# The opening's loads in one queue: weights in order of use on SyncE, a later pair on ScalarE

## Chip, cores, metric

The kernel runs on one core of one Trainium2 chip. The metric is the device time of one execution in microseconds (us); the median of three runs before the change is 1103.35 us (1103.25 to 1103.62). One more execution was profiled; times inside the kernel, counted from the start of its span, are from that one.

## The reference

One layer over x (256 tokens x 2048 features, float32): a norm, a combined projection, two kinds of attention with 8 heads each, a projection back, and a feed-forward block with a short convolution.

```python
h = rms_norm(x, attn_norm)
proj = h @ w_in                                    # 2048 x 6152
out_a = forgetting_attention(...)                  # 8 heads of 128
out_b = stick_breaking_attention(...)              # 8 heads of 128
x = x + concat(rms_norm(out_a), rms_norm(out_b)) @ w_out
u = conv3(rms_norm(x) @ w_up)
x = x + (silu(gate(u)) * val(u)) @ w_down
```

## The kernel before

Every float32 product is made of three products of a two-part split: a matrix is rounded to a high part on ScalarE or VectorE, VectorE subtracts it from the original for the low part, and TensorE adds up high by high, low by high and high by low.

The change lies in `opening()`, which computes the first 512 columns of `h @ w_in` for all 256 tokens. The weights of this product are 16 row tiles of 128 x 512 float32 (256 KB each), here called W0 to W15; x comes in column pieces of 128 features for both halves of the tokens, x0 to x15 (256 KB for two of them). The product runs in eight steps, c = 0 to 7; step c uses the weight tiles 2c and 2c+1 and the x pieces of the same numbers.

`load_x(k, n)` (L90) issues one DMA for the pieces k to k+n-1, always on SyncE's (SP's) queue. `load_w(c, which, queue)` (L391) issues one DMA for the pair c, or for one tile of it where `which` is given, on SP's queue or the queue named. Three buffers `w_raw` hold two pairs each: W0 to W3, W4 to W7, W8 to W11, then the first again.

`keep_busy(n)` (L379) issues n matmuls of zeros into a bank that nothing reads. `columns` (L126) turns the norm's weights, 16 x 128 in `prow`, into one value for each partition (`ga`): a transpose on TensorE and a copy on VectorE. `transposed_split` (L133) transposes x pieces on TensorE; ScalarE scales them by `ga` into the high part of `hT` (L143) and VectorE makes the low part (L146). `split_w(c)` (L402) makes `w_hi` and `w_lo` of pair c. In step 0 each tile is taken by itself: W0's cast is VectorE's (L409), W1's is ScalarE's (L418). In step 1 VectorE casts both tiles (L415); from step 2 on ScalarE casts the pair at once (L418). All `w_lo` are VectorE's (L419). `multiply(c, i, n, high)` (L423) issues the matmuls (L428): eight with the high weights for a pair, then four with the low ones.

The order of TensorE, VectorE, ScalarE and SP in the opening is that of the code (`manual_schedule`, L476): on each engine, instructions stand as the program issues them, and each engine runs its own in order. A DMA issue is an instruction of the queue's engine, so one on ScalarE stands between its casts. A DMA signals its end on one of eight semaphores, which are given out in turn; when all eight have been used, the next issue also waits until the earlier transfer with its semaphore has landed.

After the opening come the other projection columns by `token_major` (L237), whose weights go through the same three buffers on SP's queue (L200), attention, and the feed-forward block.

Of the kernel before, what the change touches and what calls it, by code (L numbers as in the profile page):

```python
# [18 lines left out]
KT = D // P  # L19
# [26 lines left out]
def hybrid_layer(  # L46
# [19 lines left out]
    nc = tc.nc  # L66
# [11 lines left out]
    def f32(t):  # L78
        return t.bitcast(F32)
# [4 lines left out]
    prow = const.tile([50, P], F32, name="prow")  # L84
# [5 lines left out]
    def load_x(k, n):  # L90
        nc.sync.dma_start(x2[:, :, k * P : (k + n) * P], xp[:, :, k * P : (k + n) * P])
# [29 lines left out]
    ga = const.tile([P, KT], F32, name="ga")  # L121
# [4 lines left out]
    def columns(dst, rows, n):  # L126
        pp = psb.tile([P, 512], F32, name="pp", tag="t")
        nc.tensor.transpose(pp[:, :n], rows, ident[:n, :n])
        dve.tensor_copy(dst, pp[:, :n])
# [3 lines left out]
    def transposed_split(k, g, n=2):  # L133

        ps = psb.tile([P, 2, S], F32, name="ps_x", tag="t")
        for j in range(n):
            for t in range(NT):
                nc.tensor.transpose(  # L138
                    ps[:, j, t * P : (t + 1) * P], xt[t][:, (k + j) * P : (k + j + 1) * P], ident
                )  # L140
        for j in range(n):
            i = k + j
            act.activation(hT[:, i, 0, :], ps[:, j, :], AF.Identity, scale=g[:, i : i + 1])  # L143
        for j in range(n):
            i = k + j
            dve.scalar_tensor_tensor(  # L146
                hT[:, i, 1, :], ps[:, j, :], g[:, i : i + 1], f32(hT[:, i, 0, :]),
                op0=ALU.mult, op1=ALU.subtract,
            )

    def sums_of_squares(ss, c, tiles=range(NT)):

        for t in tiles:
            junk = late.tile([P, 512], F32, name="junk", tag="raw", bufs=4)
            act.activation(junk, xt[t][:, c * 512 : (c + 1) * 512], AF.Square, accum_out=ss[:, t, c : c + 1])
# [62 lines left out]
    def rows_of(w, k0, n, c0, cols):  # L218
        return w[k0 * P : (k0 + n) * P, c0 : c0 + cols].rearrange("(k p) c -> p k c", p=P)
# [14 lines left out]
    def of_half(h, part, t):  # L234
        return h[:, part, t * P : (t + 1) * P]
# [51 lines left out]
    with ExitStack() as actx:  # L287
# [91 lines left out]
        def keep_busy(n):  # L379
            for _ in range(n):  # L380
                nc.tensor.matmul(idle, zeros[:, :P], zeros, start=True, stop=True)
# [3 lines left out]
        def opening():  # L385

            acc = psa.tile([P, NT, 512], F32, name="acc", tag="acc")
            pairs = [[(0, 1), (1, 1)]] + [[(0, 2)]] * 7
            raws, parts = [], []

            def load_w(c, which=None, queue=nc.sync):  # L391

                if c == len(raws):
                    raw = wraw.tile([P, 2048], F32, name="w_raw", tag="w_raw")
                    raws.extend([raw[:, :1024], raw[:, 1024:]])
                for i, n in [(which, 1)] if which is not None else [(0, 2)]:
                    queue.dma_start(
                        raws[c][:, i * 512 : (i + n) * 512].rearrange("p (a b) -> p a b", a=n),
                        rows_of(wi, 2 * c + i, n, 0, 512),
                    )  # L400

            def split_w(c):  # L402
                hi = whi.tile([P, 2048], F32R, name="w_hi", tag="w_hi")
                lo = wlo.tile([P, 2048], F32R, name="w_lo", tag="w_lo")
                parts.append([t[:, :1024].rearrange("p (a b) -> p a b", a=2) for t in (hi, lo)])
                for i, n in pairs[c]:
                    cols = slice(i * 512, (i + n) * 512)
                    if c == i == 0:
                        dve.tensor_copy(hi[:, cols], raws[c][:, cols])  # L409
                        for k in range(2):  # L410
                            transposed_split(k, ga, 1)
                    elif c == 1:
                        for j in range(2):
                            half = slice(512 * j, 512 * (j + 1))
                            dve.tensor_copy(hi[:, half], raws[c][:, half])  # L415
                        transposed_split(2, ga)
                    else:
                        act.copy(hi[:, cols], raws[c][:, cols])  # L418
                    dve.tensor_tensor(  # L419
                        lo[:, cols], raws[c][:, cols], f32(hi[:, cols]), op=ALU.subtract  # L420
                    )

            def multiply(c, i, n, high):  # L423
                hi, lo = (p[:, i : i + n] for p in parts[c])
                order = [(j, l, hi) for j in range(n) for l in range(2)] if high else [(j, 0, lo) for j in range(n)]
                for m, (j, l, r) in enumerate(order):
                    for t in range(NT):
                        nc.tensor.matmul(  # L428
                            acc[:, t, :], of_half(hT[:, 2 * c + i + j], l, t), r[:, j, :],
                            start=high and c == i == m == 0, stop=not high and c == 7 and m == n - 1,  # L430
                        )

            load_x(0, 2)
            nc.scalar.dma_start(prow[:KT, :], attn_norm[0].rearrange("(n p) -> n p", p=P))
            act.preload_act_table_set("natural_log_exp_and_others")
            load_w(0, 0)
            load_w(0, 1, nc.scalar)
            load_x(2, 2)
            load_w(1, 0, nc.scalar)
            load_w(1, 1)  # L440
            load_x(4, 2)
            load_w(2)
            load_x(6, 2)
            load_w(3)
            load_x(8, 4)
            load_w(4)
            load_x(12, 4)
            load_w(5)
            keep_busy(14)
            columns(ga, prow[:KT, :], KT)  # L450
            split_w(0)
            keep_busy(4)

            def behind(c):
                if c:
                    transposed_split(2 * c + 2, ga)
                split_w(c + 1)

            multiply(0, 0, 1, True)
            multiply(0, 1, 1, True)  # L460
            behind(0)
            sums_of_squares(ss1, 0, [0])
            multiply(0, 0, 1, False)
            multiply(0, 1, 1, False)
            for c in range(1, 8):
                if c < 7:
                    behind(c)
                sums_of_squares(ss1, c // 2, [c % 2])
                if c == 2:
                    load_w(6)  # L470
                    load_w(7)
                multiply(c, 0, 2, True)
                multiply(c, 0, 2, False)
            return acc

        with tc.high_priority(offset=AHEAD), tc.manual_schedule(  # L476
            engines={mybir.EngineType.PE, mybir.EngineType.DVE, mybir.EngineType.Activation, mybir.EngineType.SP}
        ):
            acc_q0 = opening()
# [695 lines left out]
```

## Time and profile before

| | |
|---|---|
| median of three runs | 1103.35 us |
| the profiled execution | 1103.81 us |
| its span | 1102.0 us |
| TensorE matmul busy | 1096.5 us (99%) |
| VectorE / ScalarE / GpSimd busy | 877.7 / 701.9 / 44.4 us |
| chain that ended last | PE 99% |
| data moved | 245.89 MB, 223 GB/s over the span |

The rows name an engine (PE is TensorE, PEld its weight loads, DVE VectorE, ACT ScalarE, POOL GpSimd, SP SyncE; SPq and ACTq are DMA issues), a line of the kernel, the operation and its operands, written tile first. An idle time in brackets lies just ahead of a row's first instruction, with what ended it. Numbers ahead of an engine are its start and its length in us. Rows of stretches give, for each engine, the busy time and the number of instructions, then the granted TensorE clock (1.00 is full), the DMA engines' mean busy share and the GB/s that they moved.

### The profile page before, as it was taken

How to read it: one execution, taken by the hardware profiler on the slowest of the kernel's cores; microseconds unless marked ns; L12 is line 12 of the kernel's file. 1: busy time of each engine (PE TensorE's matmuls, PEld its weight loads, DVE VectorE, ACT ScalarE, POOL GpSimd, SP SyncE). 2: the span in 40 equal slices, each digit the busy share in tenths (PEclk: the TensorE clock that was granted, in tenths of full speed). 3: DMA queues.
4: the chain of work that ended last, by engine and by line, in shares of the span. 5: the costliest groups of instructions: out<-in, count | busy, mean ns of one | idle time of the engine just before them, and what ended most of it. 6: DMA issues, size and time to landing. Idle time of an engine off the chain costs nothing.

```text
span 1102.0 us, 14826 instructions
## 1 busy us (share of the span) xinstructions
PE 1096.5 (99%) x5868; PEld 951.2 (86%) x5868; DVE 877.7 (80%) x941; ACT 701.9 (64%) x879; POOL 44.4 (4%) x46
## 2 busy tenths in 40 slices
PE   9999999999999999999999999999999999999998
PEld 7998888888888888888888888888888888888887
DVE  5655777975775677689889988889798889889896
ACT  6544556664653566677767776767676777677753
POOL 0000000000000000000000010100000010100010
PEclk9999999999999999999999999999999999999999
DMA  8776654576545396558989597986979689997985
GB/s 288 171 244 230 188 156 153 153 231 197 184 161 186 112 317 196 181 191 209 288 223 312 191 234 264 261 269 177 315 209 303 217 218 282 241 266 198 322 208 177
DMA packets 179407, 245.89 MB, mean 223 GB/s; under 512 B 4432, under 2 KB 119018, under 8 KB 179082
## 3 DMA queue, kind: packets, MB, share of 16 engines
q1 hardware_dynamic: 162458, 209.67, 58.6%
q0 software_dynamic: 16560, 34.75, 16.8%
q8 instruction: 46, 0.75, 0.3%
q10 hardware_dynamic: 320, 0.53, 0.1%
q14 instruction: 23, 0.19, 0.0%
HBM read 242.82 MB, written 2.11 MB: 222 GB/s over the span
## 4 chain that ended last, share of the span: by engine, by line
PE 99%; DMA 0%; DVE 0%; SPq 0%; issue 0%
PE pu L254 34%; PE acc L229 22%; PE pu L260 18%; PE bank_a L229 10%; PE bank_b L229 5%; PE bank_c L229 2%; PE acc L428 2%; PE acc L1053 1%; PE ps_x L138 1%; PE ps_o L593 1%; PE bank_a L1053 1%; PE ps_p L607 0%; DMA w_raw<-in_w_in_dram 0%; PE ps_o L594 0%; PE ps_h L307 0%; PE ps_s L522 0%
## 5 line engine op out<-in xcount | busy, mean ns | idle before, releaser
L208 DVE TENSOR_TENSOR w_lo<-w_raw,w_hi 128x2048 fp32r<-128x2048 f32 (+1 forms) x196 | 439.6, 2246 | 129.5 <-ACT w_hi L207 128.6
L207 ACT CAST w_hi<-w_raw 128x2048 fp32r<-128x2048 f32 (+1 forms) x196 | 367.3, 1877 | 235.9 <-PE acc L229 66.6
L254 PE MATMUL pu<-hT,w_hi 128*128 128x512 f32 x1664 | 394.0, 390 | 0.0
L254 PEld LDWEIGHTS pu<-hT,w_hi 128*128 128x128 f32 x1664 | 310.3, 188 | 63.2
L260 PEld LDWEIGHTS pu<-hT,w_lo 128*128 128x128 f32 x1664 | 211.9, 191 | 7.0
L260 PE MATMUL pu<-hT,w_lo 128*128 128x256 f32 x1664 | 215.1, 283 | 0.0
L229 PE MATMUL acc<-w_hi,hT 128*128 128x512 f32 (+1 forms) x576 | 124.5, 368 | 0.0
L229 PEld LDWEIGHTS acc<-w_hi,hT 128*128 128x128 f32 x576 | 101.5, 188 | 14.3
L207 ACT CAST w_hi<-w_sum 128x2048 fp32r<-128x2048 f32 x30 | 57.3, 1909 | 44.2 <-PE pu L254 36.6
L208 DVE TENSOR_TENSOR w_lo<-w_sum,w_hi 128x2048 fp32r<-128x2048 f32 x30 | 68.7, 2290 | 20.8 <-ACT w_hi L207 20.7
L870 ACT ACTIVATE tap<-up,ccol 128x256 f32<-128x256 f32 x176 | 74.6, 495 | 0.0
L229 PE MATMUL acc<-w_lo,hT 128*128 128x512 f32 (+1 forms) x288 | 64.6, 366 | 0.0
L229 PEld LDWEIGHTS acc<-w_lo,hT 128*128 128x128 f32 x288 | 51.6, 188 | 7.5
L975 POOL DMA_DIRECT2D w_sum<-in_w_down_dram x20 | 25.7, 1284 | 797.7 <-DVE w_lo L208 786.1
L229 PE MATMUL acc<-w_hi,oT 128*128 128x512 f32 x192 | 46.0, 392 | 0.0
L229 PEld LDWEIGHTS acc<-w_hi,oT 128*128 128x128 f32 x192 | 35.7, 188 | 7.3
L229 PE MATMUL bank_a<-w_hi,g 128*128 128x512 f32 x160 | 40.0, 392 | 0.0
L229 PE MATMUL bank_b<-w_hi,s 128*128 128x512 f32 x160 | 40.0, 392 | 0.0
L229 PE MATMUL bank_a<-w_hi,s 128*128 128x512 f32 x160 | 40.0, 392 | 0.0
L229 PEld LDWEIGHTS bank_b<-w_hi,s 128*128 128x128 f32 x160 | 28.9, 189 | 5.2
L229 PEld LDWEIGHTS bank_a<-w_hi,g 128*128 128x128 f32 x160 | 28.8, 189 | 5.3
L229 PEld LDWEIGHTS bank_a<-w_hi,s 128*128 128x128 f32 x160 | 28.9, 189 | 5.2
(211 smaller groups left out, 1068.7 us busy)
## 6 DMA issues: line engine op xcount, KB each, us to landing
w_raw<-in_w_up_dram SPq DMA_DIRECT2D x88, 1024.0 KB, 7.5
w_raw<-in_w_down_dram SPq DMA_DIRECT2D x44, 1024.0 KB, 6.4
w_raw<-in_w_in_dram SPq DMA_DIRECT2D x36, 1024.0 KB, 5.4
w_sum<-in_w_down_dram POOLq DMA_DIRECT2D x20, 1024.0 KB, 9.9
w_raw<-in_w_out_dram SPq DMA_DIRECT2D x16, 1024.0 KB, 5.1
w_raw<-in_w_down_dram POOLq DMA_DIRECT2D x10, 1024.0 KB, 14.9
w_raw<-in_w_in_dram SPq DMA_DIRECT2D x12, 688.0 KB, 4.2
w_raw<-in_w_in_dram SPq DMA_DIRECT2D x6, 512.0 KB, 6.8
```

The source lines that it names most:

```text
L138: nc.tensor.transpose(ps[:, j, t * P : (t + 1) * P], xt[t][:, (k + j) * P : (k + j + 1) * P], ident)
L207: act.copy(hi[:, :n], raw[:, :n])
L208: dve.tensor_tensor(lo[:, :n], raw[:, :n], f32(hi[:, :n]), op=ALU.subtract)
L229: nc.tensor.matmul(o, lhs(i, l, t), r[:, i, :], start=starts and j == 0, stop=stops and j == 3 * n - 1, skip_group_check=more,)
L254: nc.tensor.matmul(acc[:, j, :], hi[:, i, j * P : (j + 1) * P], hT[:, k].rearrange("p a b -> p (a b)"), start=k == 0, stop=low_first and k ...
L260: nc.tensor.matmul(acc[:, j, S:], lo[:, i, j * P : (j + 1) * P], hT[:, k, 0, :], start=False, stop=not low_first and k == KT - 1,)
L428: nc.tensor.matmul(acc[:, t, :], of_half(hT[:, 2 * c + i + j], l, t), r[:, j, :], start=high and c == i == m == 0, stop=not high and c == ...
L593: nc.tensor.matmul(po, v[j][:, hs], wp[:, k], start=i == 0, stop=False)
L870: act.activation(taps[w][:, j, :], u[:, j, w : w + S], AF.Copy, scale=ccol[:, w, f : f + 1])
L975: nc.gpsimd.dma_start(mem[into][:, : nk * 512].rearrange("p (a b) -> p a b", a=nk), src, accum_op=ALU.add)
L1053: nc.tensor.matmul(o, of_half(g, l, t), r[:, i, c0 : c0 + cols], start=kh == 0 and j == 0, stop=kh == n - 1 and j == 11,)
```

## The change

Only the order of the opening's loads, their queues and one idle matmul are changed. W1 and W2 go from ScalarE's queue to SP's, in the order in which they are used. The pair W4, W5 goes from SP's queue to ScalarE's, and its issue is moved behind ScalarE's part of step 0. The norm's weights stay the first issue of ScalarE's queue. `keep_busy(4)` ahead of the first product becomes `keep_busy(3)`.

```diff
-            load_x(0, 2)
             nc.scalar.dma_start(prow[:KT, :], attn_norm[0].rearrange("(n p) -> n p", p=P))
             act.preload_act_table_set("natural_log_exp_and_others")
+            load_x(0, 2)
             load_w(0, 0)
-            load_w(0, 1, nc.scalar)
+            load_w(0, 1)
             load_x(2, 2)
-            load_w(1, 0, nc.scalar)
+            load_w(1, 0)
+            load_x(4, 2)
             load_w(1, 1)
-            load_x(4, 2)
-            load_w(2)
             load_x(6, 2)
+            keep_busy(14)
+            columns(ga, prow[:KT, :], KT)
+            split_w(0)
+            keep_busy(3)
+            load_w(2, queue=nc.scalar)
             load_w(3)
             load_x(8, 4)
             load_w(4)
             load_x(12, 4)
             load_w(5)
-            keep_busy(14)
-            columns(ga, prow[:KT, :], KT)
-            split_w(0)
-            keep_busy(4)
```

SP's instructions before, from the first load on. The 128x2x256 rows are x0-1, x2-3, x4-5 and x6-7; the 128x512 rows W0 and W3; then come W4-5, x6-7, W6-7, x8-11, W8-9, x12-15 and W10-11. DMAHW0 to 7 are the eight semaphores (the ending is the same in every row):

```order
L91 DMA x_73<-in_x_dram 128x2x256
L397 DMA w_raw<-in_w_in_dram 128x512
L91 DMA x_73<-in_x_dram 128x2x256
L397 DMA w_raw<-in_w_in_dram 128x512
L91 DMA x_73<-in_x_dram 128x2x256
L397 DMA w_raw<-in_w_in_dram 128x2x512 [waits DMAHW0_49]
L91 DMA x_73<-in_x_dram 128x2x256 [waits DMAHW1_49]
L397 DMA w_raw<-in_w_in_dram 128x2x512 [waits DMAHW2_49]
L91 DMA x_73<-in_x_dram 128x2x512 [waits DMAHW3_49]
L397 DMA w_raw<-in_w_in_dram 128x2x512 [waits DMAHW4_49]
L91 DMA x_73<-in_x_dram 128x2x512 [waits DMAHW5_49]
L397 DMA w_raw<-in_w_in_dram 128x2x512 [waits DMAHW6_49]
```

The same place on SP after the change: x0-1, W0 and W1, x2-3, W2, x4-5, W3, x6-7, W6-7, x8-11, the weights of the second norm, W8-9.

```order
L91 DMA x_73<-in_x_dram 128x2x256
L397 DMA w_raw<-in_w_in_dram 128x512 x2
L91 DMA x_73<-in_x_dram 128x2x256
L397 DMA w_raw<-in_w_in_dram 128x512
L91 DMA x_73<-in_x_dram 128x2x256
L397 DMA w_raw<-in_w_in_dram 128x512
L91 DMA x_73<-in_x_dram 128x2x256 [waits DMAHW0_49]
L397 DMA w_raw<-in_w_in_dram 128x2x512 [waits DMAHW1_49]
L91 DMA x_73<-in_x_dram 128x2x512 [waits DMAHW2_49]
L101 DMA prow<-in_ffn_norm_dram 16x128 [waits DMAHW3_49]
L397 DMA w_raw<-in_w_in_dram 128x2x512 [waits DMAHW5_49]
```

W1 now stands ahead of x2-3, W2 ahead of x4-5 and W3 behind it, and W4-5 is gone from the queue; seven issues instead of five stand ahead of the first that waits.

ScalarE before, from the norm's weights to the cast of the pair W4-5 (128x1024):

```order
L434 DMA prow<-in_attn_norm_dram 16x128
L435 ACT_TABLE_LOAD
L397 DMA w_raw<-in_w_in_dram 128x512 x2
L143 ACTIVATE hT<-ps_x,ga 128x256 [waits DVE_49,PE_49]
L143 ACTIVATE hT<-ps_x,ga 128x256 [waits PE_49]
L418 CAST w_hi<-w_raw 128x512 [waits DMAHW4_49]
L143 ACTIVATE hT<-ps_x,ga 128x256 [waits PE_49]
L143 ACTIVATE hT<-ps_x,ga 128x256
L155 ACTIVATE junk,ss_116<-x_73 128x512 [waits DMAHW3_49,DMAHW1_49]
L143 ACTIVATE hT<-ps_x,ga 128x256 [waits PE_49]
L143 ACTIVATE hT<-ps_x,ga 128x256
L418 CAST w_hi<-w_raw 128x1024 [waits DMAHW0_49,DVE_49]
```

ScalarE after, the same place:

```order
L433 DMA prow<-in_attn_norm_dram 16x128
L434 ACT_TABLE_LOAD
L143 ACTIVATE hT<-ps_x,ga 128x256 [waits DVE_49,PE_49]
L143 ACTIVATE hT<-ps_x,ga 128x256 [waits PE_49]
L418 CAST w_hi<-w_raw 128x512 [waits DMAHW3_49]
L397 DMA w_raw<-in_w_in_dram 128x2x512 [waits DMAHW4_49]
L143 ACTIVATE hT<-ps_x,ga 128x256 [waits PE_49]
L143 ACTIVATE hT<-ps_x,ga 128x256
L155 ACTIVATE junk,ss_116<-x_73 128x512 [waits DMAHW1_49]
L143 ACTIVATE hT<-ps_x,ga 128x256 [waits PE_49]
L143 ACTIVATE hT<-ps_x,ga 128x256
L418 CAST w_hi<-w_raw 128x1024 [waits DMAHW4_49,DVE_49]
```

The issues of W1 and W2 are gone from ScalarE's start. That of W4-5 stands behind the cast of W1 and waits for x2-3, whose semaphore it takes.

## The prediction, on record before the changed kernel ran

> **What bounds the kernel now.** I read the page's first part, then TensorE's waits, then the stretches between them. TensorE has hardly any idle time, and the view of its waits over the whole span has three rows (who waited, for whom, us in all, times, longest):
>
> ```profile
> span 1102.0 us, 14826 instructions
> PE 1096.5 (99%) x5868; PEld 951.2 (86%) x5868; DVE 877.7 (80%) x941; ACT 701.9 (64%) x879; POOL 44.4 (4%) x46
> PE idle L381 <- DVE zeros L371: 1.1, 1, 1.1
> PE acc L428 <- DVE w_hi L409: 1.1, 1, 1.1
> PE ps_x L138 <- DMA x<-in_x_dram: 0.2, 1, 0.2
> ```
>
> All three lie ahead of the first real product. The stretches say the same:
>
> ```profile
> 6.59:31.90 25.31, 25.30 (x124) 20.54 (x125) 18.65 (x30) 18.21 (x39) 0.00 (x0) 1.00 0.79 271
> 31.90:1098.60 1066.70, 1066.70 (x5723) 927.73 (x5721) 857.73 (x909) 681.24 (x838) 43.27 (x38) 1.00 0.76 223
> ```
>
> From 6.59 to 1098.6 us TensorE has work in every moment at a granted clock of 1.00. So the time is the start of the first product, plus a block of TensorE work that the change doesn't touch, plus a tail. What the change can give is an earlier start than 6.59; what it can cost is a new hole in the opening. The chain to that start is one transfer and one cast:
>
> ```profile
> 1.23 4.77 DMA w_raw<-in_w_in_dram
> 6.00 0.02 issue
> 6.02 0.44 DVE w_hi L409
> 6.46 0.14 issue
> 6.59 2.06 PE acc L428 x8
> ```
>
> W0 is issued at 1.23, lands at 6.00, is cast, and TensorE starts 0.59 us after the landing.
>
> **The change: the weights' order.** Now the DMA stretches (last two columns: share and GB/s) and the issues with their time to landing (W0; W1 and W2 together; x2-3; W6-7):
>
> ```profile
> 1.50:2.50 1.00, 1.00 (x6) 0.72 (x5) 0.00 (x0) 1.00 (x1) 0.16 (x2) 1.00 0.50 92
> 2.50:3.50 1.00, 1.00 (x7) 0.73 (x5) 0.00 (x0) 0.01 (x1) 0.00 (x0) 1.00 0.95 233
> 3.50:4.50 1.00, 0.80 (x6) 0.37 (x4) 0.17 (x1) 0.00 (x0) 0.00 (x0) 1.00 1.00 334
> 4.50:5.50 1.00, 1.00 (x8) 0.73 (x8) 0.00 (x0) 0.57 (x2) 0.00 (x0) 1.00 0.93 254
> 5.50:6.50 1.00, 0.04 (x1) 0.00 (x0) 0.48 (x2) 0.52 (x2) 0.00 (x0) 1.00 1.03 351
> 6.50:7.50 1.00, 0.91 (x4) 0.81 (x5) 1.00 (x3) 0.36 (x1) 0.00 (x0) 1.00 1.00 333
> 7.50:8.50 1.00, 1.00 (x7) 0.75 (x6) 1.00 (x3) 0.00 (x0) 0.00 (x0) 1.00 1.07 390
> 8.50:18.00 9.50, 9.50 (x51) 7.83 (x50) 6.83 (x12) 7.22 (x17) 0.00 (x0) 1.00 1.05 384
> ...
> w_raw<-in_w_in_dram SPq DMA_DIRECT2D x1, 256.0 KB, 4.8
> ...
> w_raw<-in_w_in_dram ACTq DMA_DIRECT2D x2, 256.0 KB, 5.9
> x<-in_x_dram SPq DMA_DIRECT2D x1, 256.0 KB, 6.0
> ```
>
> The DMA engines are full from 2.5 us on, so a transfer lands when those ahead of it have been moved. Adding up the stretches, 92, 325, 659, 913, 1264, 1597 and 1987 KB have been moved by 2.5, 3.5, ... 8.5 us. One 256.0 KB transfer is 262 KB in these units; the norm's weights add 8. W0 and W1, with x0-1 ahead of them, make 794 KB, reached at 5.03, and W0 landed at 6.00: 1.0 later. x2-3 is the fifth (W2 beside it): 1319 KB, reached at 6.67, landed at 1.74 + 6.0 = 7.74: 1.1 later. So I estimate each landing as the time of its bytes plus 1.05 us.
>
> In the new order only x0-1 stands ahead of W0, and nothing shares the engines with these two but 8 KB. The second transfer's 532 KB are reached at 4.12, so W0 lands at about 5.2 instead of 6.0; I take 5.25, **a gain of 0.75** at the first product. Bounds: at least 0, since no byte ahead of W0 is added; at most 1.2, since the idle time was 1.05 and one idle matmul of 0.15 is taken out (four took 0.60):
>
> ```profile
> 4.95 0.60 PE L381 MATMUL idle<-zeros 128*128 128x256 bf16 x4
> 6.59 2.06 PE L428 MATMUL acc<-w_hi,hT 128*128 128x512 f32 x8 [1.05 <-DVE w_hi L409]
> ```
>
> That matmul itself gives nothing: it ended at 5.55, well ahead of the product.
>
> By the same sum W1 lands at 6.1, x2-3 at 7.0, W2 at 7.7, x4-5 at 8.5 and W3, the seventh, at 9.1 (1842 KB at 8.13). What needs them:
>
> ```profile
> 6.24 0.62 ACT L418 CAST w_hi<-w_raw 128x512 fp32r<-128x512 f32 x1 [0.48 <-DMA w_raw<-in_w_in_dram]
> 8.35 0.76 DVE L415 CAST w_hi<-w_raw 128x512 fp32r<-128x512 f32 x2
> 10.00 0.88 DVE L146 SCALAR_TENSOR_TENSOR hT<-ps_x,ga,hT 128x256 fp32r<-128x256 f32 x2 [0.90 <-ACT hT L143]
> 10.80 1.21 DVE L419 TENSOR_TENSOR w_lo<-w_raw,w_hi 128x1024 fp32r<-128x1024 f32 x1
> ...
> 12.07 0.76 PEld L428 LDWEIGHTS acc<-w_lo,hT 128*128 128x128 f32 x4 [0.17 <-DVE w_lo L419]
> 12.16 1.10 PE L428 MATMUL acc<-w_lo,hT 128*128 128x512 f32 x4
> ```
>
> W1's cast would end at 6.75; its product is the fifth matmul of the row of eight, at about 5.85 + 1.0, so it is just in time. W3 is **late next**: before, it had landed when VectorE came to it at 8.35. Now the chain from its landing to the low product of step 1 is a cast of 0.42, 0.80 to the next start, 1.21 for `w_lo` and 0.15 to TensorE, with 0.02 at the start: 2.60. From 9.1 this gives 11.7 instead of 12.16. So the gain that passes this point is 0.46, and the rest of the 0.75 becomes a wait here.
>
> **The change: W4-5 on ScalarE's queue.** Its issue waits for x2-3 (7.0) behind W1's cast. Behind it on ScalarE stands the scaling of x2-3, which TensorE's transposes release only at 9.13 before, so the issue of about 0.45 us is hidden; if TensorE were earlier by more than 1.6 us it would not be.
>
> ```profile
> 10.42 0.33 SPq L101 DMA_DIRECT2D prow<-in_out_norm_fox_dram  x1
> 1.25 0.94 ACTq L397 DMA_DIRECT2D w_raw<-in_w_in_dram  x2
> 9.13 0.84 ACT L143 ACTIVATE hT<-ps_x,ga 128x256 fp32r<-128x256 f32 x2 [2.27 <-PE ps_x L138]
> 11.24 1.05 ACT L418 CAST w_hi<-w_raw 128x1024 fp32r<-128x1024 f32 x1
> 13.46 0.71 PE L428 MATMUL acc<-w_hi,hT 128*128 128x512 f32 x2
> ```
>
> Before, W4-5 had landed by 10.42, where SP's next issue had waited for it, and TensorE took it at 13.46. Landing, 1.05 of cast and 0.15 more make it usable, so with TensorE 0.46 earlier (13.0) it must land by 11.8. By how the two queues shared before, W0 and W1 were issued within 0.02 us of each other on the two queues and landed at 6.00 and before 6.24, so they got about equal parts. Issued at 7.0, W4-5 runs beside x6-7 and at most half of W6-7: 10 to 11 transfers of 262 KB, reached at 10.2 to 10.9, landed at 11.2 to 11.9. I take 11.5, the middle: no wait. The end of the range costs 0.1.
>
> The Trainium skill, "DMA: Bandwidth & Descriptors", section "Queues, rings and completion order", says that each DMA engine goes round robin between the queues that have work, packet by packet. The equal landings of W0 and W1 agree. Its section "Issuing engines are not separate DMA queues" says that issuing from several engines saves only issue time; by that rule W1 and W2 lose nothing on SP's queue but their early place, and W4-5 gains nothing on ScalarE's. Both leave the sum as it is.
>
> The rest is at nothing. The two issues taken from ScalarE's start (0.94) lay in its idle time. The waits of SP's later issues fall on other transfers, but its queue stays full until W10-11 lands at about 17.9, as before, with the same bytes. Behind this, loads wait for buffers that VectorE frees, and these move with TensorE.
>
> **Sum.** 1102.04 - 0.46 = 1101.6 of span; the profiled execution was 1103.81, so 1103.35 for its like. Its time lies 0.46 above the median, so for the median I take off the same: 1103.35 - 0.45 = **1102.9**.
>
> **The rivals.**
> 1. W0's gain is whole, because W3 too lands early: the first transfers may be moved faster when only one queue is served (254 GB/s between 4.5 and 5.5, with both queues, is the lowest after the start). W0 at 5.2 and W3 at 8.8: 0.75 off, 1102.6. Against it: x0-1 alone, in the stretch to 3.5, got no more than 233.
> 2. The gain is eaten in the opening or never arises: W3 at 9.5 leaves 0.06; or W0's pace is set by slow first packets and not by W1's, and the start stays at 6.6. 1103.2 to 1103.4. For it: my lag of 1.05 is fitted on two landings, and 0.4 decides.
> 3. Slower: W4-5 on ScalarE's queue is not served in equal parts but behind SP's backlog. It costs from a landing at 12.26 on (13.46 less 1.2), us for us. Served last, it lands at 17.9, where the whole backlog ended:
>
> ```profile
> 17.92 0.36 SPq L103 DMA_DIRECT2D cs<-in_cst_dram  x1
> ```
>
> This makes the product start at 19.1 instead of 13.46: 5.6 more, 1109.0. Against it: W1 was served beside SP's queue at once. By the Trainium skill, "DMA: Bandwidth & Descriptors", "Queues, rings and completion order", an engine may drain a packet of many descriptors from one queue before it turns to the other; no run here shows how W4-5 would fare by that.
>
> **How the numbers follow.** The forecast has 0.62, rival 1 has 0.13, rival 2 has 0.17, rival 3 has 0.08, most of it (0.05) a landing only a little late, at 1103.4 to 1104. The range goes from 1102.4, somewhat beyond rival 1, to 1103.7, which takes in rival 2 and a late W4-5 of 0.3. A difference of 0.2%, 2.2 us, is about what a measurement of this kernel can tell from no change; all TensorE idle time ahead of the first product is 2.3 us, so faster by that has 0.01, slower 0.03 (rival 3 far out), within it 0.96.
>
> **What would show it.** In the changed profile the wait ahead of L428 should shrink from 1.05 to about 0.4 and the first product start at about 5.85. The wait for `w_lo` L419 at step 1's low product should grow from 0.17 to about 0.4, with VectorE's L415 rows apart and waiting for a DMA. ScalarE's cast of 128x1024 in step 2 should start at about 11.5, with a DMA as releaser. I am wrong if the first product still starts after 6.4, or if TensorE waits for ScalarE in step 2.

## The result and the profile after

| | before | after |
|---|---|---|
| median (six executions each, same chip) | 1103.3 us (1103.15 to 1103.62) | 1106.86 us (1106.28 to 1108.88) |
| ratio, 95% interval | | 1.0036 [1.0023, 1.0048] |
| profiled execution / its span | 1103.81 / 1102.0 us | 1107.15 / 1105.4 us |

The change costs 3.6 us by the medians, where 0.4 less was forecast. It is slower by more than the 0.2% that a measurement can tell, and outside the predicted range.

The page's first two lines of after, and the view of TensorE's waits over the whole span:

```profile
span 1105.4 us, 14823 instructions
...
PE 1097.8 (99%) x5867; PEld 951.3 (86%) x5867; DVE 878.1 (79%) x941; ACT 702.8 (64%) x879; POOL 44.4 (4%) x46
```

```profile
PE acc L428 <- ACT w_hi L418: 2.8, 2, 2.5
PE idle L381 <- DVE zeros L371: 1.1, 1, 1.1
PE acc L428 <- DVE hT L146: 0.4, 1, 0.4
```

The wait for W0's cast (1.1 before) is gone. In its place stand two waits for a cast of ScalarE's, 2.8 in all, and one for `hT`. Where they lie, TensorE's timeline of after tells (start, length, then the idle time just ahead, with what ended it):

```profile
5.75 1.18 PE L428 MATMUL acc<-w_hi,hT 128*128 128x512 f32 x4
7.32 1.19 PE L428 MATMUL acc<-w_hi,hT 128*128 128x512 f32 x4 [0.39 <-ACT w_hi L418]
...
10.14 0.71 PE L428 MATMUL acc<-w_hi,hT 128*128 128x512 f32 x2
11.21 1.63 PE L428 MATMUL acc<-w_hi,hT 128*128 128x512 f32 x6 [0.35 <-DVE hT L146]
12.73 1.20 PE L428 MATMUL acc<-w_lo,hT 128*128 128x512 f32 x4
...
16.82 2.12 PE L428 MATMUL acc<-w_hi,hT 128*128 128x512 f32 x8 [2.46 <-ACT w_hi L418]
```

Read beside the rows of before. The first product starts at 5.75 instead of 6.59: 0.84 won. The second half of it waits 0.39 for W1's cast. Step 1's low product starts at 12.73 instead of 12.16: 0.57 behind by now. Step 2 starts at 16.82 instead of 13.46, 3.36 behind, and nothing is won or lost after that: the last matmul of the program starts 3.33 later than before. Step 2's wait for ScalarE's cast is 2.46 of it; most of the rest stood already in step 1.

The chain of work that ended last, inside the first 25 us of after, leads to that wait:

```profile
2.20 6.00 DMA x<-in_x_dram
...
8.22 7.42 DMA w_raw<-in_w_in_dram
...
15.72 1.05 ACT w_hi L418
...
16.82 3.03 PE acc L428 x12
```

Two transfers in series: x2-3, issued at 2.20, lands at 8.20; only then is W4-5 issued on ScalarE's queue, since it takes x2-3's semaphore, and it is on its way for 7.42 us. The forecast was 7.0 for the issue and 11.5 for the landing; it landed at 15.65.

### The profile page after: what moved, and what is told of

The parts are those of the page before. It is cut to its first block, busy times and chain, and to the rows that moved or that the text cites. A ratio compares the mean times of both kernels' runs of the same rounds, so it can differ in the third digit from the quotient of the medians.

```text
span 1105.4 us, 14823 instructions
## 1 busy us (share of the span) xinstructions
PE 1097.8 (99%) x5867; PEld 951.3 (86%) x5867; DVE 878.1 (79%) x941; ACT 702.8 (64%) x879; POOL 44.4 (4%) x46
## 4 chain that ended last, share of the span: by engine, by line
PE 98%; DMA 1%; SPq 0%; ACT 0%; DVE 0%; issue 0%; ACTq 0%
PE pu L254 34%; PE acc L229 22%; PE pu L260 18%; PE bank_a L229 10%; PE bank_b L229 5%; PE bank_c L229 2%; PE acc L428 2%; PE acc L1053 1%; DMA w_raw<-in_w_in_dram 1%; DMA x<-in_x_dram 1%; PE ps_o L593 1%; PE bank_a L1053 1%; PE ps_p L607 0%; PE ps_x L138 0%; PE ps_o L594 0%; PE ps_h L307 0%
```

## The experiments

Each comparison ran beside the kernel before on the same chip; its median there was 1103.38 to 1103.53.

| run | edit | median us (range, executions) | ratio [95%] | W4-5 issued, landed | step 2 starts |
|---|---|---|---|---|---|
| e1_sp_same_place | after, W4-5 on SP | 1104.14 (1103.8 to 1104.74, 11) | 1.0006 [0.9997, 1.0015] | 4.67, 11.88 | 13.61 |
| e4_w45_alone | before, W4-5 alone moved to ScalarE | 1105.86 (1105.3 to 1108.59, 9) | 1.0024 [1.0014, 1.0033] | 8.66, 15.43 | 16.60 |
| e8_sp_late | after, W4-5 on SP, later | 1106.89 (1105.67 to 1108.41, 7) | 1.003 [1.0019, 1.004] | 6.41, 14.15 | 15.32 |
| e11_earlier_issue | after, W4-5 on ScalarE, earlier | 1105.79 (1105.44 to 1106.65, 11) | 1.0021 [1.0012, 1.003] | 6.75, 14.22 | 15.40 |
| e5_empty_queue | after, x6-7 and what follows held back | 1106.53 (1106.11 to 1107.33, 8) | 1.0027 [1.0017, 1.0038] | 9.81, 14.69 | 15.97 |
| e2_act_early | after, W4-5 on ScalarE at the start | 1104.92 (1104.75 to 1106.57, 11) | 1.0016 [1.0007, 1.0025] | 1.26, 6.06 | 14.55 |
| e3_order_alone | after, W4-5 on SP ahead of x6-7 | 1104.2 (1103.55 to 1105.56, 11) | 1.0007 [0.9998, 1.0015] | | 13.34 |
| e6_w1_on_act | e3 with W1 on ScalarE | 1103.46 (1103.11 to 1105.16, 11) | 1.0001 [0.9992, 1.001] | | 13.19 |
| e10_after_again | after, unedited | 1108.08 (1106.92 to 1108.44, 5) | 1.004 [1.0027, 1.0052] | 7.74, 15.02 | 16.19 |
| e9_busy_in_hole | after, idle matmuls ahead of step 2 | 1106.35 (1105.91 to 1107.2, 10) | 1.0022 [1.0013, 1.0032] | 7.95, 15.24 | 16.42 |

One execution of e11 took 5399.69 us, of which no profile tells the cause; it is left out of the row. In e5 it is x6-7, landed at 15.45, that step 2 waited for. The last two columns are of the profiled execution. Not every expectation was met: the medians of e1, e2, e3 and e8 lie 0.1, 0.4, 0.7 and 0.7 us above the ranges given with theory A or A1, e3 had none of the waits expected, e4's first product came at 5.97 instead of 6.6, and in e10 four of five executions were high instead of one to three of ten.

### Is it W4-5's move?

The pair back on SP's queue, at the same place in the program:

```diff
-            load_w(2, queue=nc.scalar)
+            load_w(2)
```

> The changed kernel, but W4-5 is issued on SP's queue at the same place of the code (behind x6-7, ahead of W6-7). Theory A (the issue on ScalarE comes at 8.22, behind x2-3's landing, when x6-7, W6-7 and x8-11 are already queued on SP): W4-5 is issued near 4.7, lands with the tenth transfer of 256 KB at about 11.5 to 12.4, step 2 starts at about 13.0 to 13.6 instead of 16.82, and the median is 1103.3 to 1104.0. Theory B (the new order of W1 to W3 makes most of the loss): the median stays above 1105.5.

And the counterpart, the kernel before with this move alone:

```diff
-            load_w(2)
             load_x(6, 2)
+            keep_busy(14)
+            columns(ga, prow[:KT, :], KT)
+            split_w(0)
+            keep_busy(4)
+            load_w(2, queue=nc.scalar)
             load_w(3)
...
-            keep_busy(14)
-            columns(ga, prow[:KT, :], KT)
-            split_w(0)
-            keep_busy(4)
```

> Only the second part of the change, on the kernel before: W1 and W2 stay on ScalarE's queue, W4-5 goes to ScalarE's queue behind the cast of W1. Theory A: the first product starts at 6.6 as before, W4-5 is issued after 8 and lands at 14 to 16, step 2 waits 2 us or more; the median is 1105.5 to 1107.5. Theory B: 1103.3 to 1104.

e1 takes 2.7 us off the changed kernel, and e4 alone adds 2.4 to the kernel before. ScalarE's timeline of e1 has the pair's cast at 11.96, close to the 11.5 that was forecast for it in the changed kernel:

```profile
11.96 1.05 ACT L418 CAST w_hi<-w_raw 128x1024 fp32r<-128x1024 f32 x1 [1.21 <-DMA w_raw<-in_w_in_dram]
```

In ScalarE's timeline of e4 it starts at 15.50, after 4.23 us of idle time:

```profile
15.50 1.04 ACT L418 CAST w_hi<-w_raw 128x1024 fp32r<-128x1024 f32 x1 [4.23 <-DMA w_raw<-in_w_in_dram]
```

So the move of W4-5 makes most of the loss, and the order of the other weights is not needed for it. What e1 still lies above the kernel before, 0.7 us, is not told from none.

### The queue, or the time of the issue?

Three runs move the issue. e8 leaves it on SP's queue, but behind x8-11 (its first two lines only let the pairs be issued out of order):

```diff
-                if c == len(raws):
+                if c >= len(raws):
...
-            load_w(2, queue=nc.scalar)
             load_w(3)
             load_x(8, 4)
+            load_w(2)
             load_w(4)
```

> The changed kernel, but W4-5 is issued on SP's queue behind x6-7, W6-7 and x8-11, which is what was queued on SP when ScalarE issued it. Theory A1 (the backlog ahead of it is the price): W4-5 lands as the fourteenth transfer of 256 KB, at 13.8 to 14.6, against 15.65 on ScalarE's queue; step 2 starts at 15.0 to 15.8; median 1105.0 to 1106.2. Rival C (the queue of ScalarE is the price): W4-5 lands near 12.4 and the median is within 0.5 of 1104.1.

e11 leaves it on ScalarE's, ahead of W1's cast:

```diff
                         for k in range(2):
                             transposed_split(k, ga, 1)
+                        load_w(2, queue=nc.scalar)
...
-            load_w(2, queue=nc.scalar)
```

> The changed kernel with W4-5's issue on ScalarE ahead of W1's cast instead of behind it. It then takes W1's semaphore and waits for W1 (landed 6.63) instead of x2-3 (8.20), so it is issued 1.6 us earlier, at about 6.6, again after x6-7, W6-7 and x8-11 (issued 4.18 to 5.64 on SP's queue). If ScalarE's queue were served beside SP's from the issue on, the landing would come 1.6 earlier too, at about 14.0, and step 2 would start at about 15.2. If the transfer has to wait until what SP's queue was given before has been moved, the landing stays within 0.5 of 15.65, TensorE's wait in step 2 stays at 2 us or more, and the median at 1106.3 to 1108. W1's cast starts 0.4 later in either case, at about 7.05, which adds some 0.4 to the wait for it and changes nothing behind step 2.

e2 puts it at the start of ScalarE's queue, where no semaphore has been used up:

```diff
             load_w(1, 1)
+            load_w(2, queue=nc.scalar)
             load_x(6, 2)
...
-            load_w(2, queue=nc.scalar)
```

> The changed kernel, but W4-5 is issued on ScalarE's queue right behind the norm's weights, ahead of ScalarE's part of step 0; its semaphore makes it wait only for these weights (landing at 3.5). Theory A (lateness of the issue): W4-5 lands by 11, step 2 no longer waits for it; its 512 KB come between the first tiles, so W1 to W3 land up to 1.4 later and step 0 or 1 waits more; the median is 1103.3 to 1104.5. Rival C (ScalarE's queue itself is served late, about 7.4 us from issue to landing wherever it stands): W4-5 lands at 11 to 12 and W1 to W3 are not delayed; the median is 1102.8 to 1103.3. Theory B: above 1105.5.

The chains of e8 and of e11 read alike, though one queue is SP's and the other ScalarE's (in e11 the lines behind L411 are one higher):

```profile
6.41 7.74 DMA w_raw<-in_w_in_dram
...
14.23 1.05 ACT w_hi L418
...
15.32 3.02 PE acc L428 x12
```

```profile
1.74 4.99 DMA w_raw<-in_w_in_dram
...
6.75 7.47 DMA w_raw<-in_w_in_dram
...
14.30 1.05 ACT w_hi L419
...
15.40 3.06 PE acc L429 x12
```

From issue to landing the pair takes 7.2 (e1) and 7.7 us (e8) on SP's queue, and 6.8 (e4), 7.3 (e10), 7.3 (e9), 7.4 (after) and 7.5 us (e11) on ScalarE's, in all runs that issue it between 4.6 and 8.7 us. **The queue makes no difference to the way that these runs can tell; the time of the issue sets the landing.** The profiles carry this better than the medians: e8's seven executions spread over 2.7 us, and their median lies 1.1 above e11's, though step 2 starts within 0.08 us of e11's in the profiles.

e11's issue is 1.47 us earlier than after's, its landing 1.43 earlier, and step 2 1.42. On SP's own queue the way may still be the backlog ahead of it: e8 landed at 14.15, where that theory had put it (13.8 to 14.6). For ScalarE's queue my theory in e11, that the transfer waits for all that SP's queue was given before, falls: the landing moved with the issue, and W4-5 even landed ahead of x8-11 (14.22 against 14.78), which had been issued 1.2 us before it. The other case put in e11, that both queues are served side by side from the issue on, isn't what happens either. ScalarE's queue moved its first packet of W4-5 3.2 us after the issue in after, 3.6 in e11, and 2.4 to 3.7 in the other runs that issue it there at 7.7 or later with SP's queue full; from then on the two queues share. Why an empty queue waits that long, none of these runs shows. The view of DMA queues of after, from 11.4 to 15 us (q1 is SP's, q10 ScalarE's; packets, MB, share of the 16 engines):

```profile
q1 hardware_dynamic: 478, 0.86, 65.4%
q10 hardware_dynamic: 271, 0.52, 39.1%
```

By the Trainium skill, "DMA: Bandwidth & Descriptors", section "Issuing engines are not separate DMA queues", DMAs of all issuing engines interleave on the same 16 DMA engines, and issuing from several saves only issue time. The 7.2 to 7.7 us on SP's queue beside 6.8 to 7.5 on ScalarE's agree.

What is it that makes 7 us of a transfer of 512 KB? In e5 SP's queue has little to do when W4-5 is issued, because x6-7 and everything behind it is held back until VectorE is through with step 0 (small loads of parameters stand ahead of it on SP's queue, so x6-7 is issued at 10.07):

```diff
-            load_x(6, 2)
             keep_busy(14)
             columns(ga, prow[:KT, :], KT)
             split_w(0)
+            dve.memset(x2[:, 0, 6 * P : 6 * P + 1], 0.0)
+            load_x(6, 2)
             keep_busy(3)
```

> The changed kernel, but SP's x6-7 and all pairs behind it are held back: VectorE writes one column of x6-7's buffer after the low part of W1, and the load waits for that; the small loads of parameters move ahead on SP. W4-5 stays on ScalarE's queue and now waits for a small load that lands with W3, near 9.5, so it is issued later than 8.22, with no 512 KB transfer queued on SP ahead of it. Theory A1 (of the 7.4 us from its issue to its landing, 3 and more are the backlog on SP's queue): it lands 3.5 to 5 us after its issue. Rival C (ScalarE's queue is slow by itself): again 7 us or more. The time is slower than 1104.5 either way, since the issue itself is later.

W4-5 then takes 4.9 us, with its first packet 1.05 us after the issue instead of 3.2; in e2, issued at 1.26 with little ahead of it, it takes 4.8. So some 2.5 of the 7.4 us go away where little has been given to the DMA engines before. In e2 step 2 no longer waits, but W1 lands at 7.85 and its cast is waited for, 1.6 us in step 0, so the early place has its own price. The loads that were held back cost e5 all that this saved. Stretches of e5 (busy time and instructions of PE, PEld, DVE, ACT and POOL, granted clock, DMA share, GB/s):

```profile
9.50:10.50 1.00, 1.00 (x7) 0.62 (x5) 0.43 (x1) 0.25 (x1) 0.00 (x0) 1.00 0.51 163
10.50:11.50 1.00, 0.72 (x2) 0.30 (x2) 0.38 (x1) 1.00 (x3) 0.00 (x0) 1.00 0.44 46
11.50:12.50 1.00, 0.85 (x5) 0.71 (x5) 1.00 (x3) 0.93 (x4) 0.00 (x0) 1.00 0.71 118
12.50:13.50 1.00, 1.00 (x5) 0.64 (x4) 1.00 (x3) 0.00 (x0) 0.00 (x0) 1.00 1.00 294
```

From 10.07 on loads were issued again one behind the other, and still only 46 and 118 GB/s were moved in the next two stretches, against 385 in a full one. The DMA engines were not idle in them, 0.44 and 0.71 busy. Of the 230 packets of these two us 147 were under 512 bytes; whether these small parameter loads ahead of x6-7 or a slow restart held the rate down is not shown.

### Where the earlier start went

e3 has the new order of the weights with W4-5 early on SP's queue, and e6 puts W1 back on ScalarE's queue as well:

```diff
-            load_w(0, 1)
+            load_w(0, 1, nc.scalar)
...
             load_w(1, 1)
+            load_w(2)
             load_x(6, 2)
...
-            load_w(2, queue=nc.scalar)
```

(e3 is this without its first two lines.)

> Only the first part of the change: W1 and W2 on SP's queue in order of use, W4-5 on SP behind W3 and ahead of x6-7. Theory A: the first product starts at 5.75, 0.84 earlier than before; the waits for W1 (0.4) and in step 1 (0.35) stay; no wait in step 2; the median is 1103.2 to 1103.5. Theory B: slower than 1105.

> Order of use on SP with W1 alone on ScalarE's queue: SP has x0-1, W0, x2-3, W2, x4-5, W3, W4-5, x6-7 and the rest; ScalarE's queue has the norm's weights and W1. Theory D (with one queue less is moved in the first 7.5 us, and the slowest DMA engine holds every later tile: this, not the order, gives W0's gain back in W1 and W3): W0 lands at 5.2 to 6.0, W1 within 0.4 of it, no wait for W1's cast; median 1102.9 to 1103.5. Rival E (order alone decides): the same as with all on SP, 1103.9 to 1104.3.

Neither gains. In their profiled executions the first product starts at 5.78 and 6.00 instead of 6.59, but step 2 at 13.34 and 13.19 instead of 13.46: of 0.81 and 0.59 only 0.12 and 0.27 are left. TensorE's timelines, of e3 and then of e6, show where:

```profile
5.28 0.85 PE L381 MATMUL idle<-zeros 128*128 128x256 bf16 x3
5.78 2.73 PE L428 MATMUL acc<-w_hi,hT 128*128 128x512 f32 x8
```

```profile
5.28 0.85 PE L381 MATMUL idle<-zeros 128*128 128x256 bf16 x3
6.00 2.39 PE L428 MATMUL acc<-w_hi,hT 128*128 128x512 f32 x8
```

The first eight matmuls take 2.73 and 2.39 us where before took 2.06, without a wait. Three idle matmuls take 0.85 there, where before had four in 0.60. TensorE works more slowly in these executions until some 6.7 us, though the rows' column of granted clock says 1.00; the single events of the clock in the trace reach full speed at 3.83 us in before, but at 6.90 in e3 and 6.66 in e6. The order doesn't set this: e1 issues the same seven loads first as e3 and has 3.78, and e4, which keeps the order of before there, has 5.96 where before has 3.83. It differs from execution to execution, over the twelve profiles from 3.78 to 6.90.

With the early clock, e1 shows the other way in which the gain goes. Its first product starts at 5.20, 1.39 earlier than before, but then waits for W1's cast and, in step 1, 0.36 us for `hT`; step 2 starts at 13.61:

```profile
5.20 1.21 PE L428 MATMUL acc<-w_hi,hT 128*128 128x512 f32 x4
6.86 1.20 PE L428 MATMUL acc<-w_hi,hT 128*128 128x512 f32 x4 [0.46 <-ACT w_hi L418]
```

The medians of e1 and e3 lie 0.7 and 0.8 above that of before; 0.2% is about 2.2 us, so this difference is not told from none, and nothing in the two profiles accounts for it.

In after, W1 and W3 are late as well, and in e1 W1 is waited for (0.5 us). Fewer bytes were moved there. One stretch from 1.5 to 7.5 us, of before, of after, and of e6 (busy time of PE alone, then granted clock, DMA share and GB/s):

```profile
1.50:7.50 6.00, 4.75 (x26) 1.00 0.90 266
```

```profile
1.50:7.50 6.00, 5.61 (x26) 1.00 0.79 239
```

```profile
1.50:7.50 6.00, 6.00 (x26) 1.00 0.88 284
```

With two queues at work in these 6 us, before and e6 moved 1596 and 1704 KB; with SP's alone, after moved 1434. That the number of queues is the cause isn't shown: of the other runs with SP's queue alone, six moved 242 to 251 GB/s but e5 271, and of those with two, e4 moved 285 but e2 258. In any case the transfers behind W0 come later in after than the sum had them: W1 at 6.63, W3 at 10.31.

### The higher executions

Two of the six executions of after took some 2 us more than the others (1108.4 and 1108.88), with a mean granted clock of 0.998. The unedited kernel again, and beside it one with TensorE busy in the hole:

```diff
                 if c == 2:
                     load_w(6)
                     load_w(7)
+                if c == 2:
+                    keep_busy(12)
                 multiply(c, 0, 2, True)
```

> The changed kernel once more, unedited, as the measure for the run beside it. Theory: 1106.3 to 1107.2 in most executions, and in one to three of ten about 2 us more (1108.3 to 1108.9), with a mean granted clock of 0.998. Rival, that the higher executions of the first comparison were chance: all executions within 0.5 us of each other.

> The changed kernel with twelve idle matmuls (0.15 us each, 1.8 us) ahead of step 2's high product, so that TensorE works through most of the 2.5 us in which it waits for W4-5. Theory: W4-5's landing still sets step 2's start (16.8), so the median stays where the fast executions of the changed kernel are, 1106.3 to 1106.8; but the executions at 1108.4 to 1108.9 are those in which the granted clock fell to 0.50 for 3.4 us after the wait, and with TensorE busy these go away: no execution above 1107.6. Rival: the higher executions have another cause (the clock falls at another place, or a transfer is late); then as many of them remain as in the changed kernel run beside it. A second rival, that the idle matmuls themselves delay step 2: it would then start after 16.9 with no wait ahead of it.

The profile of e10 caught such an execution. TensorE's timeline, and its stretches (length, PE's busy time and instructions, granted clock, DMA share, GB/s):

```profile
16.19 3.65 PE L428 MATMUL acc<-w_hi,hT 128*128 128x512 f32 x8 [2.29 <-ACT w_hi L418]
19.68 1.09 PE L428 MATMUL acc<-w_lo,hT 128*128 128x512 f32 x4
```

```profile
13.90:16.20 2.30, 0.01 (x2) 0.99 1.05 388
16.20:19.60 3.40, 3.40 (x8) 0.51 1.05 387
19.60:30.00 10.40, 10.40 (x53) 1.00 0.46 134
```

After 2.29 us without work the granted clock is 0.51 for 3.4 us, and the eight matmuls take 3.65 us instead of 2.12: 1.5 more. Four of five executions of e10 had a mean clock of 0.998 (1107.88 to 1108.44), two of nine of e4, two of seven of e8, and none of ten of e9, which has the same late landing:

```profile
14.05 1.47 PE L381 MATMUL idle<-zeros 128*128 128x256 bf16 x12
16.42 2.12 PE L428 MATMUL acc<-w_hi,hT 128*128 128x512 f32 x8 [0.89 <-ACT w_hi L418]
```

So the hole costs twice: its length always, and in some executions 1.5 us more for the clock that falls behind it. It isn't the length alone that decides: the profiled execution of after waited 2.46 us and kept 1.00.

The traces show what goes with it. Up to the last one, each record of the clock in them lasts 3.41 us or a whole multiple of it (10.24 is three, 1099.09 is 322), counted from where it first reached full speed, which differs as told above. So the clock moves in steps of 3.41 us that lie differently in each execution. These are the steps in which the hole lies, of e10, e4, after and e8, with the next step for e4 and after (length, PE's busy time and instructions, granted clock, DMA share, GB/s):

```profile
12.73:16.14 3.41, 1.17 (x8) 1.00 1.05 386
```

```profile
12.79:16.20 3.41, 0.86 (x6) 1.00 1.03 380
16.20:19.61 3.41, 3.01 (x7) 0.50 1.06 381
```

```profile
12.56:15.97 3.41, 1.81 (x10) 1.00 1.05 387
15.97:19.38 3.41, 2.56 (x11) 1.00 1.05 386
```

```profile
13.57:16.98 3.41, 1.66 (x7) 1.00 1.05 387
```

Behind the first two, with TensorE busy for 1.17 and 0.86 us of 3.41, the next step was granted 0.50; behind the other two, with 1.81 and 1.66, it was granted 1.00. The hole of after is split between two steps. In these four profiles, then, the place of the hole in the steps goes with the fall, and that it comes in some executions only would follow from it. Where between 1.17 and 1.66 the bound lies isn't measured. Nor is there a profile of the three of e2's eleven executions with a mean clock of 0.998 (1106.4 to 1106.57), whose longest wait in the profiled execution is 1.6 us. The Trainium skill, "TensorE: Matmul & The Clock Gate", section "HAM oscillation — how this bites in real kernels", warns of idle gaps above some 3.4 us; here 2.29 were enough in one profiled execution, and 2.46 were not in another.

## Why the prediction was wrong, step by step

- **The step that failed: "Issued at 7.0, W4-5 runs beside x6-7 and at most half of W6-7 ... landed at 11.2 to 11.9 ... I take 11.5, the middle: no wait."** It was issued at 8.22 and took 7.42 us: landed at 15.65, 4.15 late. 1.22 of this is the issue, because x2-3 landed later than its sum said; 2.92 is the way, 7.42 instead of 4.5. W0 and W1, from which equal parts had been read, were issued at the very start, with only x0-1 ahead; in a full stretch the pair takes some 7 us. SP's timeline of before had the row, which I did not use: W4-5 itself, issued at 3.91 and landed by 10.42, 6.5 us.

```profile
3.91 0.38 SPq L397 DMA_DIRECT2D w_raw<-in_w_in_dram  x1
```

- **"The end of the range costs 0.1"** followed from it. Rival 3 had the landing cost us for us from 12.26 on, and so it did: 15.65 is 3.39 behind that, and step 2 starts 3.36 later. That rival had the right sign and the right place, but not the mechanism. It let W4-5 be served behind SP's backlog, at the worst last, at 17.9; the runs show a way of some 7 us counted from the issue, on either queue. Why ScalarE's queue, empty before, moves nothing in the first 3.2 us of it stays open.
- **W0 lands at 5.25, a gain of 0.75: the gain came out near, in part by luck.** W0 landed at 4.72, 0.53 earlier than forecast: VectorE's cast of it (L409) starts at 4.74. Yet the first product started only 0.84 earlier than before, at 5.75 instead of the 5.85 forecast, and the wait ahead of it, of which 0.4 should have been left, is gone: TensorE, at full clock only from 5.73 on, was busy up to it. Two errors offset each other. In e1, with full clock from 3.78, the first product came 1.39 earlier, beyond the bound of 1.2.

```profile
4.74 0.43 DVE L409 CAST w_hi<-w_raw 128x512 fp32r<-128x512 f32 x1
...
8.90 0.43 DVE L415 CAST w_hi<-w_raw 128x512 fp32r<-128x512 f32 x1 [0.91 <-DMA w_raw<-in_w_in_dram]
10.33 0.43 DVE L415 CAST w_hi<-w_raw 128x512 fp32r<-128x512 f32 x1 [1.00 <-DMA w_raw<-in_w_in_dram]
```

- **Landing = bytes plus 1.05 us, with full DMA engines: wrong**, too late for W0 and too early for all behind it. W1 came at 6.63 (6.1 forecast), x2-3 at 8.20 (7.0), W3 at 10.31 (9.1; the sum's own terms, 8.13 and 1.05, make 9.18). 239 GB/s were moved instead of 266, and the lag grew: of the sixteen parts of x2-3 the middle one was there at 6.1 and the last at 8.2.
- **W3 is late next: right in kind, mis-sized.** The L415 rows just shown stand apart and wait for a DMA, as forecast. But the low product of step 1 started 0.57 later than before instead of 0.46 earlier; so the gain was gone ahead of step 2 already. The landing was mis-sized, by 1.2 us; the chain behind it, 2.60 in the forecast, took 2.42.
- **The block behind step 2 is untouched: right.** 3.36 us at step 2, 3.33 at the last matmul.

Without W4-5's wait the change would be e1 or e3, no difference that can be told.

## What to carry to other kernels

In a stretch with full DMA engines, read from the trace what one transfer takes from its issue to its landing there, on whichever queue, and count back from the product that needs it: here some 7 us for the 512 KB of W4-5, so an issue behind a landing at 8 feeds nothing before 15.7. Look also at which semaphore a moved issue takes: here it was W1's ahead of W1's cast (issued at 6.75, e11) and x2-3's behind it (issued at 8.22). A gain at the first product is worth nothing until every product behind it in the opening has been checked by the same sum, and a new hole in TensorE's work can cost the clock beside its length, in some executions and not in others.

## What the hardware showed that I had not expected

- From issue to landing, the 512 KB of W4-5 took 6.8 to 7.7 us on either of the two queues with the DMA engines full, and 4.8 to 4.9 us with little ahead.
- ScalarE's queue, empty before, moved the first packet of W4-5 2.4 to 3.7 us after its issue while SP's queue was full, and 1.05 us after it in e5.
- The clock moved in steps of 3.41 us that lay differently in each execution: full speed came 3.78 to 6.90 us after the span's start.
- It fell to 0.50 for one step of 3.41 us behind steps in which TensorE had been busy for 0.86 and 1.17 us, and not behind 1.66 and 1.81.
- In e5, with small loads under way and several issues waiting, 46 and 118 GB/s were moved in two successive us at a DMA share of 0.44 and 0.71, and 294 in the third.
